# Preparation of a chunked RWKV-7 recurrence: the 64-row products of both heads and both halves ahead of the transposes

## The chip, the cores and the metric

The kernel runs on one core of a Trainium2 chip. The metric is device time of one execution in microseconds. Three executions of the kernel before took 3186.7, 3193.28 and 3202.15 us; the median is 3193.28 us.

## The reference

A decoder trunk of two layers on a 1024 x 1024 input. Layer 0 mixes tokens with a gated MLP, layer 1 with an RWKV-7 recurrence; each is followed by cross-attention into 256 memory rows and a SwiGLU FFN, and every sub-layer is wrapped in RMS norms. The change lies in the recurrence of layer 1, with 16 heads of 64:

```python
def rwkv7_recurrence(r, w, k, v, a, b):
    def step(S, inp):
        r_t, w_t, k_t, v_t, a_t, b_t = inp
        sa = jnp.einsum('bhij,bhj->bhi', S, a_t)
        S = S * w_t[:, :, None, :] + sa[..., None] * b_t[:, :, None, :] + v_t[..., None] * k_t[:, :, None, :]
        return S, jnp.einsum('bhij,bhj->bhi', S, r_t)
    ...
    _, y = lax.scan(step, S0, xs)
    return jnp.moveaxis(y, 0, 1)
...
def rwkv7_time_mix(x, v_first, mix, w_rkv, w0, w1, w2, a0, a1, a2, g1, g2, k_k, k_a, r_k, ln_g, ln_b, w_o, v_res):
    xm = x[None] + xx[None] * mix[:, None, None, :]
    r, k, v = jnp.einsum('pbtc,pcd->pbtd', xm[:3], w_rkv)
    ...
    decay = jnp.exp(-jnp.exp(heads(w)))
    y = rwkv7_recurrence(rh, decay, kh, vh, -kk, kk * ah)
    ...
    return (y * g) @ w_o, v_first
```

## The kernel before

Everything is float32. The large projections split an operand into a rounded part and a remainder and run three 128x512 matmuls for one product (lines L148 to L150, called "triples" below); splitting costs a cast on ACT (L118) and a subtraction on DVE (L119).

The recurrence is cut into chunks of 64 positions and done in four batches of 256 positions. A batch goes through these stages:

- `rwkv_prep` (L1313 to L1389), once for each of four groups of channels (`pi` 0 to 3). It loads five tiles (L1325), accumulates decays on DVE (L1328), takes exponentials on ACT, and builds two operand tiles AR and BK (L1340 to L1344). Partitions 0 to 63 belong to one head of a pair, 64 to 127 to the other. A group has 8 chunks of 64, taken in two halves `q` of four. For each half and head, four products of 64 rows go into one PSUM bank (L1363), and DVE masks the bank into GA and GR with two multiplications (L1366). Four 128x128 transposes of BK go into another bank (L1370), and ACT copies it (L1371). Then GA is sent to DRAM (L1376, L1377), the values are loaded into UV (L1381), and 16 more products (L1387) follow, which ACT copies (L1388).
- `rwkv_solve`: 31 steps of two DVE operations (L1409, L1410) on what the four groups of the batch have written, read back into invA (L1399). The results go to DRAM (L1414, L1417).
- `rwkv_merge`: reads these results back (L1426 into x1, L1431 into Z) and joins them with 32x32 matmuls (L1443, L1452).
- `rwkv_chunks`: the recurrence itself (L1479, L1466), and `rwkv_post`, which normalises the outputs; its reductions are on DVE (L1531, L1544), its transposes on PE (L1553, L1560).

Batch 0 is prepared while the last half of a projection (`rwkv_cols`) runs, batch 1 while the gate projection (L1307) runs and beyond it, batches 2 and 3 between two runs of `rwkv_chunks`, beside the post-processing of the batch before. Merge b stands ahead of the preparation of batch b+1 in the source.

These functions are generators. Between two `yield`s a step is recorded, and `stagger` starts the four groups of a batch some steps apart (its second argument, 7 or 6 on L1592). A scheduler at build time then puts the recorded instructions of all stages into one order for each engine; on the chip an engine follows this order and waits at each instruction for its inputs and buffers. While batches are prepared, PSUM is split into four banks for `bank()` (used by the preparation and by the post-processing of the first two batches) and four for `bank_ck()` (merge and chunks).

Of the kernel before, what the change touches and what calls it, by code (L numbers as in the profile page):

```python
# [21 lines left out]
class Trunk:  # L22
# [1290 lines left out]
    def rwkv_prep(self, R, B, pi, b, d, C):  # L1313
# [13 lines left out]
        L, kkn, b, km, r = [ld[n] for n in ('sig', 'kkn', 'b', 'km', 'r')]  # L1327
# [29 lines left out]
        for q in range(2):  # L1357
            qs = slice(q * 4, q * 4 + 4)
            for h in range(2):
                hs = slice(h * 64, h * 64 + 64)  # L1360
                ps = self.bank()
                for c in range(4):
                    nc.tensor.matmul(ps[:, c * P:(c + 1) * P], lhsT=BK[hs, q * 4 + c, :, :], rhs=AR[hs, q * 4 + c, :, :], start=True, stop=True)  # L1363
                pv = ps.rearrange('p (c a t) -> p c a t', c=4, a=2)
                for a, x in ((0, GA), (1, T['GR'])):
                    nc.vector.tensor_mul(x[:, h, qs, :], pv[:, :, a, :], self.mask[:, a].broadcast_to([P, 4, 64]))  # L1366
                yield
            ps = self.bank()
            for c in range(4):
                nc.tensor.transpose(ps[:, c * P:(c + 1) * P], BK[:, q * 4 + c, :, :], self.ident)  # L1370
            nc.scalar.copy(T['BT'][:, qs, :], ps.rearrange('p (c t) -> p c t', c=4))  # L1371
            yield
# [193 lines left out]
    def rwkv(self, W, C, filler, mk_close):  # L1566
        nc = self.nc
        B = [self.rwkv_batch() for _ in range(4)]
        R, states = ({}, {})
# [6 lines left out]
        def stagger(gens, lag):  # L1576

            gens = list(gens)
            done = [False] * len(gens)
            n = 0  # L1580
            while not all(done):
                for i, g in enumerate(gens):
                    if n >= i * lag and (not done[i]):
                        try:
                            next(g)
                        except StopIteration:
                            done[i] = True
                n += 1
                yield

        def prep(b):
            return stagger([self.rwkv_prep(R, B[b], pi, b, D_[0], C) for pi in range(4)], 7 if b else 6)  # L1592

        def chunks(b):
            yield from self.rwkv_chunks(R, B[b], b, states)
# [17 lines left out]
        D_ = []  # L1613

        def before_last():
            self.close_main()
            pools(left, 'left', ('inv', 1), ('D', 8))
            self.rwkv_consts(left.enter_context(self.tc.tile_pool(name='rconst', bufs=1, reuse_waits='tile', side='left')), C)
            pools(left, 'left', ('ld', 7))
            pools(top, 'left', ('tt', 4))  # L1620
            self.open_main(2, 3, 2)
            self.open_psum(4, 4)
            self.later(prep(0))
        d, gate_out = self.rwkv_project(W, C, filler, before_last, D_)
        self.drain()
        run(self.rwkv_solve(R, B[0]))
        p1 = prep(1)
        self.later(p1)
        gate_out()
# [11 lines left out]
        for b in range(1, 4):  # L1641
            o = 3
            sv = self.rwkv_solve(R, B[b])
            if o in (0, 1):
                run(sv, chunks(b - 1))
            elif o in (2, 3):
                run(chunks(b - 1), sv)
            else:
                self.later(sv)
                run(chunks(b - 1), rate=1)  # L1650
                self.drain(0)
            self.later(post(b - 1), 1)
            if b == 3:
                break
            if o in (0, 2, 4):
                run(self.rwkv_merge(R, B[b]))
            run(prep(b + 1), rate=1)
            if o in (1, 3, 5):
                run(self.rwkv_merge(R, B[b]))
            self.drain()  # L1660
# [99 lines left out]
```

## Time and profile before

| what | value |
|---|---|
| median of three executions | 3193.28 us |
| the profiled execution, whole | 3190.62 us |
| its span in the profile | 3188.9 us |
| mean granted clock of TensorE | 0.969 |
| first and last L1363 product | 1689.9 and 2057.7 us |

A line of groups reads: line of the code, engine, operation, tile written <- tiles read, shapes, count, then busy time and mean duration, then the engine's idle time just before these instructions and what ended it. A float32 matmul leaves two records, so 8 records of L1363 are four products. A line of the timeline gives a start, the time to the end of the last merged record, the instruction, and in brackets the idle time ahead of it with what ended it. A line of windows gives a stretch and its length, then for each engine the busy time and number of records, then the granted clock (1.00 is full), the busy share of the DMA engines and GB/s.

### The profile page before, as it was taken

How to read it: one execution, taken by the hardware profiler on the slowest of the kernel's cores; microseconds unless marked ns; L12 is line 12 of the kernel's file. 1: busy time of each engine (PE TensorE's matmuls, PEld its weight loads, DVE VectorE, ACT ScalarE, POOL GpSimd, SP SyncE). 2: the span in 40 equal slices, each digit the busy share in tenths (PEclk: the TensorE clock that was granted, in tenths of full speed). 3: DMA queues.
4: the chain of work that ended last, by engine and by line, in shares of the span. 5: the costliest groups of instructions: out<-in, count | busy, mean ns of one | idle time of the engine just before them, and what ended most of it. 6: DMA issues, size and time to landing. Idle time of an engine off the chain costs nothing. (4 is left out here: it accounts for less than half of the span.)

```text
span 3188.9 us, 43900 instructions
## 1 busy us (share of the span) xinstructions
PE 3076.4 (96%) x16570; PEld 2519.2 (79%) x16570; DVE 1826.3 (57%) x2610; ACT 1484.8 (47%) x2751; POOL 796.7 (25%) x632
## 2 busy tenths in 40 slices
PE   8999999989999999999989999999999999999998
PEld 6888888778888877878767778787788778888877
DVE  5553544565555576655765665664545655555666
ACT  5443544533333345766653344455544633333443
POOL 0100011345555200111421120323011355554101
PEclk9999999999999999999998888899999999999999
DMA  5622535423333643744867632633643423333634
GB/s 191 207 79 67 195 116 166 163 73 100 100 102 100 234 160 131 226 125 147 263 194 197 187 94 81 174 97 128 206 152 130 148 93 108 103 100 106 228 125 142
DMA packets 434580, 457.60 MB, mean 143 GB/s; under 512 B 77696, under 2 KB 309280, under 8 KB 434368
## 3 DMA queue, kind: packets, MB, share of 16 engines
q1 hardware_dynamic: 427456, 429.62, 42.4%
q0 software_dynamic: 6912, 25.17, 2.5%
q8 instruction: 131, 2.15, 0.3%
q14 instruction: 81, 0.66, 0.1%
HBM read 332.48 MB, written 122.22 MB: 143 GB/s over the span
## 5 line engine op out<-in xcount | busy, mean ns | idle before, releaser
L461 PE MATMUL ps<-a,wh 128*128 128x512 f32 x2464 | 773.1, 399 | 7.8 <-DVE a L119 7.4
L119 DVE TENSOR_TENSOR wl<-wr,wh 128x1024 fp32r<-128x1024 f32 (+1 forms) x417 | 486.1, 1176 | 458.9 <-ACT wh L118 454.5
L118 ACT CAST wh<-wr 128x1024 fp32r<-128x1024 f32 (+1 forms) x417 | 371.1, 901 | 601.4 <-PE ps L671 168.1
L461 PEld LDWEIGHTS ps<-a,wh 128*128 128x128 f32 x2464 | 466.4, 190 | 123.2 <-DVE a L119 9.2
L461 PE MATMUL ps<-a,wl 128*128 128x512 f32 x1232 | 480.7, 398 | 0.9 <-DVE wl L119 0.9
L148 PE MATMUL ps<-a,wh 128*128 128x512 f32 (+1 forms) x848 | 329.5, 393 | 9.7 <-ACT a L118 7.4
L149 PE MATMUL ps<-a,wh 128*128 128x512 f32 (+1 forms) x848 | 326.3, 386 | 2.4 <-DVE a L119 2.4
L148 PE MATMUL ps<-wh,a 128*128 128x512 f32 x800 | 314.9, 402 | 13.4 <-ACT t L1201 4.0
L150 PE MATMUL ps<-a,wl 128*128 128x512 f32 (+1 forms) x848 | 325.3, 385 | 2.3 <-DVE wl L119 2.2
L149 PE MATMUL ps<-wl,a 128*128 128x512 f32 x800 | 318.8, 399 | 0.5 <-DVE wl L119 0.5
L150 PE MATMUL ps<-wh,a 128*128 128x512 f32 x800 | 316.7, 399 | 0.0
L220 POOL TENSOR_TENSOR sm<-sm,mhalf 128x2 f32<-128x2 f32 (+3 forms) x68 | 70.8, 1045 | 902.8 <-DVE sm L240 827.0
L461 PEld LDWEIGHTS ps<-a,wl 128*128 128x128 f32 x1232 | 233.4, 189 | 57.8 <-DVE wl L119 1.3
L119 DVE TENSOR_TENSOR wl<-s,wh 128x512 fp32r<-128x512 f32 (+1 forms) x188 | 201.6, 1087 | 73.9 <-ACT wh L118 70.8
L671 PE MATMUL ps<-wl,wh 128*128 128x512 f32 x588 | 231.6, 394 | 11.5 <-DVE wl L119 11.3
L671 PE MATMUL ps<-wh,wl 128*128 128x512 f32 x588 | 230.0, 391 | 0.0
L118 ACT CAST wh<-s 128x512 fp32r<-128x512 f32 (+1 forms) x188 | 115.5, 633 | 207.9 <-PE ps L461 75.2
L148 PEld LDWEIGHTS ps<-a,wh 128*128 128x128 f32 x848 | 162.6, 193 | 43.7 <-ACT a L118 8.4
L671 PE MATMUL ps<-wh 128*128 128x512 f32 x588 | 194.3, 391 | 0.0
L150 PEld LDWEIGHTS ps<-a,wl 128*128 128x128 f32 x848 | 163.0, 193 | 37.1 <-DVE wl L119 4.0
L148 PEld LDWEIGHTS ps<-wh,a 128*128 128x128 f32 x800 | 151.7, 190 | 50.7 <-ACT t L1201 4.5
L149 PEld LDWEIGHTS ps<-a,wh 128*128 128x128 f32 x848 | 163.4, 193 | 33.0 <-DVE a L119 2.7
(289 smaller groups left out, 5284.7 us busy)
## 6 DMA issues: line engine op xcount, KB each, us to landing
scr<-a SPq DMA_DIRECT2D x218, 256.0 KB
wr<-in_ffn_w_in SPq DMA_DIRECT2D x92, 512.0 KB
wr<-scr SPq DMA_DIRECT2D x70, 512.0 KB
scr<-t SPq DMA_DIRECT2D x58, 512.0 KB
wr<-in_rw_w_rkv SPq DMA_DIRECT2D x48, 512.0 KB
a<-in_ffn_w_out SPq DMA_DIRECT2D x36, 512.0 KB
ld<-scr SPq DMA_DIRECT2D x72, 256.0 KB
t<-scr SPq DMA_DIRECT2D x34, 512.0 KB
```

Source lines behind the costliest of these rows:

```text
L118: self.nc.scalar.copy(hi, src)
L119: (engine or self.nc.vector).tensor_sub(lo, src, hi)
L148: nc.tensor.matmul(out, lhsT=ah, rhs=bh, start=start, stop=False)
L149: nc.tensor.matmul(out, lhsT=ah, rhs=bl, start=False, stop=False)
L150: nc.tensor.matmul(out, lhsT=al, rhs=bh, start=False, stop=stop)
L220: self.nc.gpsimd.tensor_tensor(out=r, in0=v, in1=self.mhalf[:, 0:n], op=ALU.pow)
L461: self.nc.tensor.matmul(out, lhsT=a, rhs=b, start=start and k == 0 and (i == 0), stop=k == 3 and i == 2, skip_group_check=True)
L671: nc.tensor.matmul(ps, lhsT=a, rhs=b, start=i in (1, 2, 5) and n == 0 and k == 0 and z == 0, stop=n == NS - 1 and k == steps[n][1] - 1 and ...
```

## The change

Two edits. The `yield` between the two heads of a half goes out of the loop over heads, and the loop over halves is cut in two: first the products of both halves, one step each with both heads, then the transposes of both halves, one step each. A group so has two steps fewer, and the distance between groups in `stagger` goes from 7 and 6 steps to 6 and 5. No instruction is added or taken away.

```diff
@@ rwkv_prep
                 pv = ps.rearrange('p (c a t) -> p c a t', c=4, a=2)
                 for a, x in ((0, GA), (1, T['GR'])):
                     nc.vector.tensor_mul(x[:, h, qs, :], pv[:, :, a, :], self.mask[:, a].broadcast_to([P, 4, 64]))
-                yield
+            yield
+        for q in range(2):
+            qs = slice(q * 4, q * 4 + 4)
             ps = self.bank()
             for c in range(4):
                 nc.tensor.transpose(ps[:, c * P:(c + 1) * P], BK[:, q * 4 + c, :, :], self.ident)
@@ rwkv
         def prep(b):
-            return stagger([self.rwkv_prep(R, B[b], pi, b, D_[0], C) for pi in range(4)], 7 if b else 6)
+            return stagger([self.rwkv_prep(R, B[b], pi, b, D_[0], C) for pi in range(4)], 6 if b else 5)
```

Behind L1367 a line of the changed kernel has a number higher by 2 (the transposes L1370 are L1372 there, the merge products L1443 are L1445). The scheduler's order changes on every engine, from the preparation of batch 0 on. Three places show it.

On PE, the third group of batch 3 before the change, from its first small products on (`ck` with L1452 is the merge of the batch before, `bk` and `ar` are BK and AR):

```order
L1351 MATMUL ps<-sel,ld 128x2 x4
L1387 MATMUL ps<-uv,bk 64x64 x7
L1363 MATMUL ps<-ar,bk 128x128 x8
L1370 MATMUL ps<-ident,bk 128x128 x4
L1452 MATMUL ck<-z_14071,x1t 32x32 x2
L1452 MATMUL ck<-z_14072,x1t 32x32
L1363 MATMUL ps<-ar,bk 128x128 x4
L1452 MATMUL ck<-z_14072,x1t 32x32
L1452 MATMUL ck<-z_14071,x1t 32x32
L1363 MATMUL ps<-ar,bk 128x128 x4
```

and the same group after it:

```order
L1389 MATMUL ps<-uv,bk 64x64 x16
L1351 MATMUL ps<-sel,ld 128x2 x4
L1363 MATMUL ps<-ar,bk 128x128 x16
L1372 MATMUL ps<-ident,bk 128x128 x4
L1454 MATMUL ck<-z_14133,x1t 32x32
L1454 MATMUL ck<-z_14134,x1t 32x32 x2
L1454 MATMUL ck<-z_14133,x1t 32x32
L1372 MATMUL ps<-ident,bk 128x128 x4
```

What was a row of 8 products (both heads of a half) and two rows of 4 (one head each) is one row of 16. Over the whole program there are 28 rows of 4 and 18 of 8 before, so 18 places where four products of one head stand next to four of the other. After, there are 40 such places; by batch they go from 5, 5, 4, 4 to 11, 9, 8, 12.

On DVE, the solve of batch 0 before the change, where the preparation of batch 1 cuts in:

```order
L1409 TENSOR_TENSOR invP<-invZ,invA 128x135
L1410 TENSOR_TENSOR invZ<-invZ,invP 128x5x27
L1340 SCALAR_TENSOR_TENSOR ar<-ld,tt 128x8x63
L1341 TENSOR_SCALAR ar<-ld 128x8
L1342 TENSOR_TENSOR ar<-ld,tt 128x8x64
L1343 TENSOR_TENSOR bk<-ld,tt 128x8x64
L1409 TENSOR_TENSOR invP<-invZ,invA 128x156
```

and after it:

```order
L1412 TENSOR_TENSOR invZ<-invZ,invP 128x11x21
L1411 TENSOR_TENSOR invP<-invZ,invA 128x240
L1340 SCALAR_TENSOR_TENSOR ar<-ld,tt 128x8x63
L1341 TENSOR_SCALAR ar<-ld 128x8
L1342 TENSOR_TENSOR ar<-ld,tt 128x8x64
L1412 TENSOR_TENSOR invZ<-invZ,invP 128x12x20
```

Five of the 31 steps stood ahead of the first operand of batch 1; now eleven and a half do. On PE, the 16 last products of batch 0 (L1387) had 75 matmuls of triples behind them before the gate projection; now they have 99.

On PE, the first merge before the change (L1307 is the last of the gate projection, `x_14093` the solve's result as read back into x1):

```order
L1307 MATMUL ps<-a 128x512
L1363 MATMUL ps<-ar,bk 128x128 x4
L1370 MATMUL ps<-ident,bk 128x128 x4
L1387 MATMUL ps<-uv,bk 64x64 x16
L1443 MATMUL ck<-x_14093 32x32 x64
L1351 MATMUL ps<-sel,ld 128x2 x4
L1363 MATMUL ps<-ar,bk 128x128 x8
```

and after it:

```order
L1307 MATMUL ps<-a 128x512
L1389 MATMUL ps<-uv,bk 64x64 x8
L1351 MATMUL ps<-sel,ld 128x2 x4
L1363 MATMUL ps<-ar,bk 128x128 x8
L1445 MATMUL ck<-x_14155 32x32
L1363 MATMUL ps<-ar,bk 128x128 x8
L1445 MATMUL ck<-x_14155 32x32 x63
L1372 MATMUL ps<-ident,bk 128x128 x8
```

The merge now has the first products (L1351) and the first half of the third group of batch 1 ahead of it; before, it came first. In batch 3 the merge now stands behind the whole product blocks of two groups, where it stood behind half a block of the first. In batch 2 it stands directly behind the product block of the first group, ahead of the transposes of the post-processing, of which three rows came first before.

## The prediction

> **What bounds the kernel now.** I read the engines' shares first, then the stretches in which batches are prepared, then the preparation's instructions one by one. First the page, then windows over batch 0, batch 2, batch 3 and one piece of batch 2:
>
> ```profile
> PE 3076.4 (96%) x16570; PEld 2519.2 (79%) x16570; DVE 1826.3 (57%) x2610; ACT 1484.8 (47%) x2751; POOL 796.7 (25%) x632
> ...
> 1692.50:1750.00 57.50, 56.89 (x389) 47.53 (x389) 32.43 (x62) 20.38 (x37) 8.18 (x7) 0.89 0.74 187
> ...
> 1889.00:1956.00 67.00, 61.36 (x592) 52.39 (x592) 39.27 (x89) 23.23 (x46) 22.19 (x19) 0.64 0.56 153
> 2005.00:2058.00 53.00, 48.87 (x568) 41.63 (x568) 31.49 (x75) 18.96 (x39) 19.78 (x18) 0.77 0.72 198
> ...
> 1930.00:1960.00 30.00, 30.00 (x250) 26.80 (x251) 12.91 (x31) 10.39 (x23) 3.20 (x4) 0.60 0.41 108
> ```
>
> PE is busy 96% of the span, and nearly all of the preparation too: 56.89 of 57.5 us in batch 0, 61.36 of 67 and 48.87 of 53 in batches 2 and 3. DVE is busy 56 to 59% there. So PE's own issue sets the pace, and what it is spared counts. The granted clock matters as much: batches 2 and 3 do about the same work, and take 67 us at 0.64 and 53 us at 0.77.
>
> The groups of 1680 to 2070 us, on DVE and PE, say who waits for whom:
>
> ```profile
> L1363 PE MATMUL ps<-ar,bk 64*128 64x128 f32 x512 | 82.8, 336 | 3.1 <-DVE sm L1544 1.4 <-ACT bo L1353 1.0 <-ACT t L1308 0.6
> L1366 DVE TENSOR_TENSOR bk<-ps,mask 128x256 f32<-128x256 f32 x64 | 26.7, 417 | 64.5 <-PE ps L1363 64.4
> ...
> L1328 DVE TENSOR_TENSOR_SCAN ld<-chunk_on,ld 128x512 f32<-128x512 bf16 x16 | 19.5, 1218 | 19.9 <-DMA ld<-scr 19.9
> ```
>
> DVE is idle for 64.4 us until L1363 delivers, while L1363 itself waits 3.1 us in all. The products are what DVE waits for.
>
> **Change, part 1: two heads side by side.** PE's timeline has one block of both heads (16 records), and a block of one head (8), each with the row that starts next, first at full clock and then at half:
>
> ```profile
> 1700.06 1.71 PE L1363 MATMUL ps<-ar,bk 64*128 64x128 f32 x16
> 1701.70 0.66 PE L1370 MATMUL ps<-ident,bk 128*128 128x128 f32 x4
> ...
> 1705.52 1.16 PE L1363 MATMUL ps<-ar,bk 64*128 64x128 f32 x8
> 1706.60 1.15 PE L1387 MATMUL ps<-uv,bk 128*64 128x64 f32 x16
> ...
> 1811.31 3.10 PE L1363 MATMUL ps<-ar,bk 64*128 64x128 f32 x16
> 1814.33 1.11 PE L1370 MATMUL ps<-ident,bk 128*128 128x128 f32 x4
> ...
> 1832.07 2.08 PE L1363 MATMUL ps<-ar,bk 64*128 64x128 f32 x8
> 1834.08 0.79 PE L1479 MATMUL ck<-s,ar 128*128 128x128 f32 x2
> ```
>
> From start to next start, one head takes 1.08 us, both 1.64. Two separate blocks would take 2.16, so each neighbourhood of two heads spares 0.52 us at full clock. At half clock it is 2 x 2.01 - 3.02 = 1.00. The products use different rows of the array and overlap where the head changes; a block also enters and leaves its shape once instead of twice.
>
> The built orders have 18 such neighbourhoods before and 40 after, 6, 4, 4 and 8 more in batches 0 to 3. That the one from the second head back to the first spares the same is an assumption; no row of before has it.
> Batch 0 at a clock of 0.89: 6 x 0.52 = 3.1. For batches 2 and 3, a clock of 0.64 means 0.72 of the time at half, 0.77 means 0.46, which gives 0.87 and 0.74 us each: 4 x 0.87 = 3.5 and 8 x 0.74 = 5.9. Batch 1 I put at 0.75: 3.0. Of the first group of batches 2 and 3, two each lie beside a wait of PE for the post-processing (part 3) and bring nothing: +3.2. Sum -12.3, call it **-12**. Bounds: 0, if other waits cover all of it, and 22 x 1.00 = -22, if all runs at half clock.
>
> [...]
>
> **Part 2: the merges' waits.** L1443, asked by its line, and its first start in merges 0 and 1:
>
> ```profile
>   DMA x<-scr: 10.4, 4
> ...
> 1807.65 1.93 PE L1443 MATMUL ck<-x 32*32 32x32 f32 x128 [4.34 <-DMA x<-scr]
> ...
> 1902.35 0.55 PE L1443 MATMUL ck<-x 32*32 32x32 f32 x24 [1.96 <-DMA x<-scr]
> ...
> 1803.27 0.88 DVE L1348 SCALAR_TENSOR_TENSOR ld<-ld,pcol 128x256 f32<-128x256 f32 x2 [1.16 <-POOL bk L1344]
> ```
>
> Merge 0 waits 4.34 us for the solve's result. The solve ran here, its start released by the read-back of GA; the triples that I count in have the spacing of the last two rows:
>
> ```profile
> 1751.94 0.19 DVE L1409 TENSOR_TENSOR invP<-invZ,invA 128x31 f32<-128x31 f32 x1 [1.34 <-DMA invA<-scr]
> ...
> 1797.96 0.21 DVE L1410 TENSOR_TENSOR invZ<-invZ,invP 128x31 f32<-128x31 f32 x1
> ...
> 1709.72 0.40 PE L150 MATMUL ps<-a,wl 128*128 128x512 f32 x1
> 1709.96 0.39 PE L148 MATMUL ps<-a,wh 128*128 128x512 f32 x1
> ```
>
> In the new order 24 more matmuls of triples stand behind batch 0's last product, at 0.24 us each 5.6 us. The solve starts that much earlier against the projection, and more of its steps stand ahead of batch 1 on DVE. So the 4.34 us go. Next is the third group of batch 1, now ahead of the merge: its last operand comes from DVE at 1804.15 (1803.27 + 0.88, L1348), while PE was through at 1803.31 (1807.65 - 4.34). I keep 0.8 us and take -3.5. Merge 2 moves behind two whole blocks; I give it half of what the other two waits have left (10.4 - 4.34 - 1.96 = 4.1, about 2 each): -1. Merge 1 moves ahead of three blocks of transposes of the post-processing, which no longer cover its wait (3.3 us, by the 1.1 of such a block of four in part 3); but its solve starts earlier by what batch 1 gains. I take 0, between -2 and +3.3. Together **-4.5**, between -8.3 (4.34 + 2 + 2) and +3.3. The DMAs of GA and UV keep their places behind each group's last mask, so SP has as many issues; POOL's L1344 keeps its place ahead of the products.
>
> **Part 3: banks.** Four products now want all four banks of the pool in one go, the transposes a fifth. DVE empties a bank at this pace:
>
> ```profile
> 1745.15 0.41 DVE L1366 TENSOR_TENSOR gr<-ps,mask 128x256 f32<-128x256 f32 x1
> 1745.48 0.42 DVE L1366 TENSOR_TENSOR bk<-ps,mask 128x256 f32<-128x256 f32 x1
> 1745.82 0.41 DVE L1366 TENSOR_TENSOR gr<-ps,mask 128x256 f32<-128x256 f32 x1
> ```
>
> 0.67 us for a pair. PE makes a bank in 1.08 us, and each further one in 0.56 (1.64 - 1.08), so four in 2.76; the first is free again at about 1.7. With DVE ready there is a slack of 1 us. Where it isn't, at the start of batches 2 and 3, the post-processing's reduction holds banks already:
>
> ```profile
>   DVE sm L1544: 9.1, 4
> ...
> 1898.22 1.12 PE L1370 MATMUL ps<-ident,bk 128*128 128x128 f32 x4 [2.19 <-DVE sm L1544]
> ```
>
> The transposes wait 2.19 us there (9.1 in four places). It will be the second half's products instead. I add 1.1 us in each of the two batches, **+2**, between 0 and 4.4.
>
> **Sum:** -12 - 4.5 + 2 = -14.5 us, on the profiled execution of 3190.62 (span 3188.9) 3176. That execution lies 2.7 us under the median of 3193.28, from which the same sum gives **3179**. A measurement here tells 0.5%, 16 us, from no change, so the boundary is 3177.
>
> **Rivals.**
>
> *The clock stays up.* The half clock lasts long here: the windows show 0.60 at 1930 to 1960 with PE busy 30.00 of 30. Denser products and shorter waits may turn one stretch back to full. At 0.64, batch 2 has 48 us of half clock; half of that at full saves 24 x (1 - 1.08/2.01) = 11 us, in both batches up to 22: 3168 to 3157. Against it: products of half the array's rows and 32x32 matmuls remain. [...]
>
> *The clock falls instead.* Batch 3 in the state of batch 2 costs 67 - 53 = 14 us: 3193.
>
> *It is covered.* Loads come next: DVE waits 19.9 us for `ld<-scr` already, at L1328, and that pool doesn't grow. If faster groups only wait for their loads and the solves, part 1 is given back: about 3190. For it, the DMA share of 0.74 in batch 0; against it, DVE's 64.4 us of waiting for products.
>
> *Banks hold PE up, and the kernel is slower.* Each of the 16 groups pays the wait that the transposes paid for L1544, 9.1/4 = 2.3 us: 37 us, hence 3216. It decides from DVE being more than the 1 us of slack late in most groups, behind solve steps and operand building. If only half the groups pay, 3197. Against it: DVE is the one that waits now.
>
> **How the numbers follow.** Forecast 0.45, its own range 3168 to 3189; clock up 0.20; covered 0.20; clock down 0.05; banks 0.10. Nearly half of the forecast's own range lies beyond the boundary: faster 0.20 + 0.22 = 0.42, slower 0.10, same 0.48. The range leaves out the banks' case and a little of the clock's best: 3158 to 3200.
>
> **What would show it.** Part 1: blocks of 32 records of L1363 in about 2.8 us at full clock, some 5.0 at half, and DVE's 64.4 us of waiting shrunk. Part 2: L1443's 10.4 us of DMA waits cut by about half, the first from 4.34 to under 1. Part 3: few waits of L1363 and the transposes for L1366. The clock rivals show in the granted clock of the windows of batches 2 and 3. I am wrong if a block of 32 takes 3.3 us or more at full clock, or if waits for `ld<-scr` or L1366 grow by 10 us.

## The result and the profile after

The changed kernel takes 3209.58 us (median of 10 executions, 3192.89 to 3217.0), the kernel before 3194.47 us in the same comparison (10 executions). The ratio is 1.0054, with a 95% interval of 1.0032 to 1.0075: slower by about half a per cent, where 14.5 us less was forecast. The profiled execution took 3210.66 us (span 3208.6), 20.0 us more than that of before.

The engines' shares on the page are nearly what they were:

```profile
PE 3070.8 (96%) x16570; PEld 2519.6 (79%) x16570; DVE 1832.7 (57%) x2610; ACT 1485.1 (46%) x2751; POOL 793.6 (25%) x632
```

PE is busy 5.6 us less than before in a span that is 19.7 us longer. The difference shows where the recurrence runs. Windows from the first product L1363 to the last transpose of the post-processing (L1553, now L1555), before and after; the numbers behind the stretch are its length and PE's busy time, and further on stands the granted clock:

```profile
1689.90:2213.90 524.00, 502.79 (x4844) 423.24 (x4844) 312.06 (x759) 246.74 (x639) 115.34 (x111) 0.87 0.47 132
```

```profile
1694.80:2233.20 538.40, 494.32 (x4845) 421.33 (x4845) 315.96 (x759) 247.49 (x639) 114.89 (x111) 0.85 0.45 128
```

The stretch grew by 14.4 us. PE's idle time in it went from 21.2 us (524.00 - 502.79) to 44.1 us, and its busy time fell by 8.5 us although more of it ran at half clock: by the clock records of the two traces, 133 us of the stretch before and 157 us after. (Another 4.9 us of the 20 arose ahead of the first product, where PE's order of instructions is the same in both kernels; that part is not the change's, and the medians differ by 15.1 us.)

What PE waited for, by the waits between 1680 and 2240 us, longest first (total, times, longest), before and after:

```profile
PE ck L1443 <- DMA x<-scr: 8.1, 3, 4.3
PE ps L1370 <- DVE sm L1544: 4.2, 2, 2.2
...
PE ps L1387 <- DMA uv<-scr: 0.2, 1, 0.2
```

```profile
PE ps L1389 <- DMA uv<-scr: 25.5, 9, 5.8
PE ps L1351 <- DVE ld L1348: 5.9, 2, 4.1
PE ps L1555 <- DVE gr L1366: 4.1, 2, 3.9
```

The new first line is the largest of what is new: the products of GA with UV (L1387, now L1389) wait 25.5 us for UV's load, which they practically never did before. The same group of channels in both kernels, the last of batch 0, shows how. Timeline of before, SP's DMAs and PE (SPq is SP's queue):

```profile
1737.84 1.25 SPq L1381 DMA_DIRECT2D uv<-scr  x2
...
1743.62 1.71 PE L1363 MATMUL ps<-ar,bk 64*128 64x128 f32 x16
...
1745.93 0.86 SPq L1376 DMA_DIRECT2D scr<-bk  x2
...
1746.83 0.58 SPq L1377 DMA_DIRECT2D scr<-bk  x1
1748.42 2.08 PE L1387 MATMUL ps<-uv,bk 128*64 128x64 f32 x32
```

and after:

```profile
1747.29 2.26 PE L1363 MATMUL ps<-ar,bk 64*128 64x128 f32 x24
...
1749.29 0.58 SPq L1383 DMA_DIRECT2D uv<-scr  x1
1749.48 1.09 PE L1372 MATMUL ps<-ident,bk 128*128 128x128 f32 x8
...
1750.44 0.41 DVE L1366 TENSOR_TENSOR gr<-ps,mask 128x256 f32<-128x256 f32 x1
1750.55 0.85 SPq L1378 DMA_DIRECT2D scr<-bk  x2
1751.45 0.60 SPq L1379 DMA_DIRECT2D scr<-bk  x1
1752.09 0.63 SPq L1383 DMA_DIRECT2D uv<-scr  x1
1754.05 3.55 PE L1389 MATMUL ps<-uv,bk 128*64 128x64 f32 x32 [3.47 <-DMA uv<-scr]
```

Before, both loads of UV were issued 8.1 us ahead of the first write of GA, although the source has them behind it: the scheduler puts them there, and they land while products, masks and transposes run. After, the first load leaves 1.3 us ahead of the writes, the second behind them. The masks are through at 1750.85, and PE stands until 1754.05, 4.2 us after the first load was issued. In the trace of before, all 16 pairs of loads stand ahead of their group's writes; after, in 3 groups both do, in 6 one, in 7 none. From the end of a load's issue to the first product that reads it there were 7.7 us on the median of the 32 loads before, and under 4.2 us for 2 of them; after it is 3.5 us, and under 4.2 for 20. (4.2 is what the load above took. The nine loads that PE waited for were used 2.2 to 4.3 us after their issue, so not every load under 4.2 is one that PE waits for.)

The granted clock fell in such a wait as well. In the clock records of this trace the granted clock is 1.00 or 0.50, and every stretch between two changes of it lasts a multiple of 3.41 us (the shortest 3.41, the longest 628.05). Five such windows of the changed kernel around another of these waits (1731.6 to 1734.54, 2.94 us):

```profile
1726.63:1730.04 3.41, 3.41 (x41) 3.33 (x40) 1.63 (x6) 1.65 (x5) 0.00 (x0) 1.00 0.71 203
1730.04:1733.45 3.41, 1.56 (x13) 1.20 (x12) 3.41 (x9) 1.07 (x2) 0.00 (x0) 1.00 1.07 260
1733.45:1736.87 3.42, 2.33 (x17) 2.24 (x18) 0.90 (x3) 0.29 (x1) 0.00 (x0) 0.50 0.73 194
1736.87:1740.28 3.41, 3.41 (x9) 2.64 (x9) 1.22 (x1) 1.03 (x3) 0.00 (x0) 0.50 0.29 100
1740.28:1743.69 3.41, 3.41 (x15) 2.49 (x14) 0.17 (x1) 0.40 (x1) 0.00 (x0) 1.00 0.26 77
```

In the second window PE is busy 1.56 of 3.41 us; the next two run at 0.50, the second of them with PE busy throughout. That one holds 9 records, the window at full clock behind it 15.

### The profile page after: what moved, and what is told of

It is laid out like the page before. It is cut to its first block, busy times and chain, and to the rows that moved or that the text cites. A ratio compares the mean times of both kernels' runs of the same rounds, so it can differ in the third digit from the quotient of the medians.

```text
span 3208.6 us, 43910 instructions
## 1 busy us (share of the span) xinstructions
PE 3070.8 (96%) x16570; PEld 2519.6 (79%) x16570; DVE 1832.7 (57%) x2610; ACT 1485.1 (46%) x2751; POOL 793.6 (25%) x632
## 4 chain that ended last, share of the span: by engine, by line
PE 81%; DVE 8%; DMA 6%; ACT 2%; issue 2%; SPq 1%; POOL 1%; DVEq 0%; POOLq 0%; ACTq 0%
PE ps L461 26%; PE ps L148 11%; PE ps L150 11%; PE ps L149 11%; PE ps L671 10%; PE ck L1468 4%; DVE wl L119 2%; PE ck L1481 2%; DVE a L119 1%; PE ps L1389 1%; PE ps L1363 1%; DMA uv<-scr 1%; DMA a<-scr 1%; DMA ld<-scr 1%; PE ps L274 1%
## 5 line engine op out<-in xcount | busy, mean ns | idle before, releaser
L148 PE MATMUL ps<-wh,a 128*128 128x512 f32 x800 | 315.6, 402 | 14.4 <-DVE a L432 4.8
L149 PEld LDWEIGHTS ps<-a,wh 128*128 128x128 f32 x848 | 163.3, 193 | 33.2 <-DVE a L119 2.7
```

What stands on the lines that cost most here:

```text
L148: nc.tensor.matmul(out, lhsT=ah, rhs=bh, start=start, stop=False)
L149: nc.tensor.matmul(out, lhsT=ah, rhs=bl, start=False, stop=False)
```

## The experiments

Three theories stand in the expectations of the first eight. U: the late loads of UV are what the changed order costs. S: it is the shift of the whole order, in which waits of many kinds replace each other. H, in e1 and e2 alone: it is the longer half clock by itself. The theories 1 to 3 and M of the later runs are told in their expectations. Each kernel was timed against the kernel before on the same chip (medians of before in the four sets: 3188.86, 3190.73, 3187.52 and 3189.1 us). In the table, "late loads" are those of the 32 with under 4.2 us from issue to use, "waits for UV" are PE's in the profiled execution, and the half clock is the mean over all timed executions, 2 x (1 - mean clock) x span in each.

| kernel | median us | ratio to before, 95% interval | late loads | waits for UV, us | half clock, us |
|---|---|---|---|---|---|
| before (90 executions) | | | 2 | 0.2 | 193 |
| the change | 3209.58 | 1.0054 [1.0032, 1.0075] | 20 | 25.5 | 215 |
| e1 change, loads ahead of the products | 3196.47 | 1.0018 [0.9996, 1.0039] | 2 | 1.8 | 206 |
| e2 before, loads ahead of the products | 3195.63 | 1.0029 [1.0007, 1.0052] | 0 | 0 | 209 |
| e3 heads joined only | 3209.16 | 1.0062 [1.0041, 1.0083] | 2 | 5.0 | 229 |
| e4 loops split only | 3224.7 | 1.0103 [1.0070, 1.0136] | 16 | 15.0 | 246 |
| e5 change, loads just ahead of GA's writes | 3227.7 | 1.0111 [1.0088, 1.0135] | 14 | 19.6 | 237 |
| e6 as e1, heads alternating | 3193.17 | 1.0007 [0.9988, 1.0026] | 2 | 1.2 | 201 |
| e7 change, distances 7 and 6 | 3205.89 | 1.0039 [1.0016, 1.0061] | 16 | 8.5 | 218 |
| e8 before, distances 6 and 5 | 3229.29 | 1.0112 [1.0077, 1.0147] | 7 | 15.1 | 252 |
| e9 change, matmuls added ahead of L1389 | 3201.63 | 1.0041 [1.0019, 1.0063] | 11 | 5.6 | 166 |
| e10 change, loads between products and transposes | 3193.48 | 1.0024 [1.0005, 1.0044] | 5 | 2.8 | 208 |
| e11 as e1, distances 7 and 6 | 3212.23 | 1.0082 [1.0057, 1.0106] | 0 | 0 | 243 |
| e12 as e6, distances 7 and 6 | 3213.17 | 1.0081 [1.0059, 1.0102] | 0 | 2.1 | 238 |
| e13 before, the same matmuls added | 3213.26 | 1.0078 [1.0050, 1.0105] | 2 | 0 | 189 |
| e14 as e10, one matmul added | 3200.92 | 1.0039 [1.0015, 1.0063] | 0 | 6.1 | 180 |

### The loads moved, in both kernels (e1, e2)

```diff
+        UV = T['UV'] = self.A.tile([P, 8, 2, 64], F32, name='uv', tag='a')
+        nc.gpsimd.memset(UV[0:64], 0.0)
+        for p in range(2):
+            nc.sync.dma_start(UV[64:128, p * 4:p * 4 + 4].rearrange('i c h v -> i c (h v)'), ...)
         for q in range(2):
             qs = slice(q * 4, q * 4 + 4)
             for h in range(2):
...
             nc.sync.dma_start(B['D1'][bl, pi].rearrange('h c i t -> i (h c) t'), ga[s, :, s])
         nc.sync.dma_start(B['D4'][pi].rearrange('i h c t -> i (h c) t'), ga[0:32, :, 32:64])
-        UV = T['UV'] = ...
```

> The changed kernel with the UV tile, its memset and its two loads recorded ahead of the products instead of behind the writes of GA. Theory U (the second UV load leaves SP's queue behind the GA writes, which wait for the last mask, so that L1389 waits on PE): the waits of L1389 for uv<-scr fall from 25.5 us to under 4, PE idle in the preparation falls by about 20 us, and the time is below the kernel before by 5 to 20 us, ratio 0.994 to 0.998. Theory H (the longer half clock of TensorE alone makes the loss): the waits go, the time stays at a ratio of 1.003 or more. Theory S (any new order of the scheduler scatters by this much): no relation between the waits and the time.

> The kernel before with the same move of the UV loads. Before, L1387 waited 0.2 us for them, so theories U and H expect no change: ratio 0.997 to 1.003. Theory S expects a change of either sign of up to 0.5%.

With the loads early, the changed order is no longer told from before (1.0018), and it is not slower than the old order with the same move (1.0029). PE's waits for UV are gone but for 1.8 us. They are not the whole story: U expected 5 to 20 us less than before. The products are denser (L1367 is busy 63.8 us in e1, the same line L1363 82.8 in the kernel before), but PE's idle time in the stretch is still 37.0 us, against 44.1 in the changed kernel and 21.2 before. Other waits have taken the place of most of the 24 us. Longest waits of PE in e1 (L1370 is the masks here, L1376 the transposes):

```profile
PE ck L1445 <- DMA x<-scr: 10.9, 3, 5.3
PE ps L1376 <- DVE gr L1370: 6.4, 3, 5.5
PE ps L1389 <- DVE a L1563: 5.1, 2, 4.3
PE ps L1389 <- DVE gr L1370: 4.8, 3, 3.7
...
PE ps L1389 <- DMA uv<-scr: 1.8, 2, 1.1
```

PE now waits 11.2 us for DVE's masks and 10.9 us for the solve's result. H expected 1.003 or more for e1; its interval doesn't exclude that, and half clock fell too, from 215 to 206 us.

### Half of the change (e3, e4) and the distances alone (e7, e8)

e3 takes the `yield` out between the heads and leaves the transposes behind their half, with the new distances 6 and 5; e4 splits the loop over halves and leaves the `yield`, with the old distances 7 and 6:

```diff
# e3
-                yield
+            yield
             ps = self.bank()
...
# e4
                 yield
+        for q in range(2):
+            qs = slice(q * 4, q * 4 + 4)
             ps = self.bank()
```

> Only the first edit: both heads of a half in one step, the transposes still behind their half, distances 6 and 5. Theory U: the transposes of the second half still follow its products, and L1387 follows the transposes, as before; waits for uv<-scr stay between the two, 5 to 15 us, and the time is within 0.4% of before. If joining the heads alone makes the loss, the ratio is 1.004 or more.

> Only the second edit: all products first and the transposes behind, with a yield after each head and the distances 7 and 6 of before. Theory U: the last mask comes earlier against L1387 by a block of transposes, so the waits for uv<-scr are under 10 us; ratio 0.997 to 1.003. If moving the transposes makes the loss, waits of 15 us or more and a ratio of 1.004 or more.

It is the split that makes the loads late (16 in e4, 2 in e3). Both are slower all the same, e3 with hardly a late load. U missed in both: it expected them within 0.4 and 0.3% of before, and under 10 us of waits for UV in e4, which has 15.0. e7 is the change with the old distances between groups, e8 the kernel before with the new ones:

```diff
# e7
-            return stagger([...], 6 if b else 5)
+            return stagger([...], 7 if b else 6)
# e8
-            return stagger([...], 7 if b else 6)
+            return stagger([...], 6 if b else 5)
```

> The changed kernel with the distances between groups of before (7 and 6). If the tighter distance causes the crowding of products against the UV loads, the waits for uv<-scr fall below 12 us and the ratio to 1.002. Theory U puts the cause inside a group (products, transposes, loads in that order), so the waits stay at 15 to 30 us and the ratio at 1.003 to 1.008.

> The kernel before with the distances of the change (6 and 5) alone. A control for what a new order of the scheduler does by itself: theory U expects 0.998 to 1.003 and waits for uv<-scr under 5 us. If such a shift alone gives 1.005, scatter of the order explains the change as well as any wait does.

The distances by themselves, with no other edit, cost the kernel before 1.1%. Its waits in e8:

```profile
PE ps L1387 <- DMA uv<-scr: 15.1, 4, 6.4
PE ck L1443 <- DMA x<-scr: 9.4, 2, 6.4
```

Four long waits for UV are part of it, and half clock is 252 us, the most of all kernels. U did not expect this, S did. In the changed kernel the old distances bring no more than 0.15 points, which the intervals don't separate, although PE's waits for UV fall from 25.5 to 8.5 us in e7. U had expected 15 to 30 us there. PE's idle time in the stretch stays at 40.0 us, so other waits replaced these, as S says.

### The loads just ahead of GA's writes (e5), and the heads alternating (e6)

e5 exchanges the four lines of UV with the five of GA's writes. e6 is e1 with the products of both heads issued in turn into two banks:

```diff
+            pss = [self.bank() for _ in range(2)]
+            for c in range(4):
+                for h in range(2):
+                    hs = slice(h * 64, h * 64 + 64)
+                    nc.tensor.matmul(pss[h][:, c * P:(c + 1) * P], lhsT=BK[hs, q * 4 + c, :, :], rhs=AR[hs, q * 4 + c, :, :], start=True, stop=True)
```

> The changed kernel with the UV tile, memset and loads just ahead of the three writes of GA, at the same step; nothing else. It takes the last mask and SP's three issues (about 1.6 us) from between the products and the second UV load. Theory U: the waits of L1389 for uv<-scr fall from 25.5 us to under 10, and the ratio from 1.0054 to 1.001 to 1.003, as with the loads ahead of the products (1.0018). If the loads are late because the values themselves or the tile come late, the waits stay above 20 us and the ratio at 1.005.

> The changed kernel with the UV loads ahead of the products, and with the heads alternating product by product (h0, h1, h0, h1) into two banks instead of four of one and four of the other. If row halves overlap at every change of head, a block of 32 records takes 1.5 to 2.1 us at full clock instead of 2.75, 16 groups spare 10 to 20 us of PE, and the ratio is 0.994 to 1.000 against 1.0018 with the loads alone. If the overlap comes only from entering the block, the block stays at 2.7 us and the ratio at 1.002.

e5 was a miss: 1.0111. The scheduler kept both loads ahead of the writes in 9 groups only, in batch 0 by 1.3 to 2.6 us, and put both behind the first write in the other 7, so 14 stay late and 19.6 us of waits remain. Why it is slower than the change itself is not explained by that. e6 has the lowest ratio of all variants, and is not told from before. Alternating did make the products denser where the built order kept it. Two rows of 16 records in e6, each with the row that starts next, at full clock:

```profile
2031.54 1.71 PE L1367 MATMUL ps<-ar,bk 64*128 64x128 f32 x16
2033.18 0.24 PE L1446 MATMUL ck<-x 32*32 32x32 f32 x2
2033.36 1.17 PE L1367 MATMUL ps<-ar,bk 64*128 64x128 f32 x16
2034.45 0.22 PE L1446 MATMUL ck<-x 32*32 32x32 f32 x2
```

The first takes 1.64 us like the rows of the changed kernel: its records start at the same distances as there, so it has four products of one head and four of the other. The second takes 1.09 us: its records start in pairs 13 ns apart, one of each half as in the source. By this spacing about half of e6's 30 rows have runs of one head only, as the scheduler built them, and in all the products of e6 are busy 60.8 us, those of e1 63.8. Little of that could show in the total.

### Filling the wait (e9), its control (e13), and loads a little earlier (e10, e14)

e9 adds two matmuls per group ahead of the products that wait; their result is overwritten:

```diff
             ps = self.bank()
+            if q == 0:
+                for _ in range(2):
+                    nc.tensor.matmul(ps, lhsT=self.ident, rhs=BK[:, 0:4, :, :], start=True, stop=True)
             for c in range(4):
```

> The changed kernel, with two added matmuls of 128x512 f32 per group on TensorE right ahead of L1389's first block (their bank is overwritten by that block; they read BK and write nothing that is kept). They depend on nothing that is late, so they fill the time in which L1389 waits for its UV load. By the blocks of four 128x128 f32 records (1.08 us) I estimate 1.1 us each, 16 x 2.2 = 35 us of added work. Theory 1 (a wait also costs clock: in nine traces, every 3.41 us window at full clock with TensorE busy under half was followed by half clock): waits for uv fall from 25.5 to under 8, half clock between the first product and the last L1555 falls from 157 to 125 us or less, and of the 35 us at least 25 come back: 1.004 to 1.009 against before. Theory 2 (half clock comes from the many small products, not from the waits): waits fall too, half clock stays at 150 us or more, time 1.010 to 1.014.

e13 is the same edit in the kernel before:

> The kernel before with the same two added matmuls per group at the same place, ahead of the first block that needs UV. It has no waits for UV to fill (0.2 us). Theory 1 (in the changed kernel the fill helped because it stood in the waits): here the added work is paid in full; with half clock at 193 us per execution on the mean before, and 215 to 166 by the fill in the changed kernel, I expect 175 us or more here and 1.006 to 1.011 against before, which is over the changed kernel with the fill (1.0041). Theory 3 (full-array matmuls anywhere in this stretch hold the clock up, waits or not): half clock falls by 40 us or more here too, and the time is 1.002 to 1.006.

The added records in the view by groups (busy time, mean ns, idle time ahead), in e9 and in e13:

```profile
L1388 PE MATMUL ps<-bk,ident 128*128 128x512 f32 x64 | 33.2, 643 | 0.7 <-DVE gr L1366 0.6
```

```profile
L1386 PE MATMUL ps<-bk,ident 128*128 128x512 f32 x64 | 36.0, 692 | 0.0
```

The stretch from the first product to the last transpose of the post-processing as a window, in e9 and in e13:

```profile
1689.40:2222.70 533.30, 507.79 (x4908) 413.21 (x4909) 316.96 (x759) 248.50 (x639) 117.70 (x111) 0.91 0.45 130
```

```profile
1693.00:2232.00 539.00, 525.66 (x4906) 425.73 (x4906) 315.44 (x760) 247.46 (x638) 118.39 (x111) 0.90 0.46 128
```

The same 33 to 36 us of added matmuls cost the kernel before 24 us (1.0078) and the changed kernel nothing (1.0041 against 1.0054). Each ratio is good to some 0.2 points, 7 us. In the changed kernel they stand where PE waited: 25.5 us of waits for UV became 5.6, PE's idle time in the stretch fell from 44.1 to 25.5 us, and half clock over all executions from 215 to 166 us. In the kernel before half clock went from 193 to 189: there the added matmuls did not hold the clock up by themselves, though its one profiled execution has 0.90 in this stretch, a high one. That speaks for the waits as the source of the half clock that e9 took away; e14 speaks against it.

e10 puts the four lines of UV between the two loops, e14 adds one such matmul to e10:

> The changed kernel with the UV tile, its memset and its loads recorded between the products and the transposes: an earlier place than in the changed kernel, a later one than ahead of the products. Theory U (the late load is what the changed order costs): the median from the issue's end to the first use, 3.5 us in the changed kernel and 16.5 with the loads ahead of the products, comes to 5 to 9 us; waits for uv 3 to 12 us; time between the two, 1.001 to 1.004. Theory S (the order of the whole stretch decides, the load is one wait among others that replace each other): waits for uv fall as well, but the time stays at 1.005 or more.

> UV loads between products and transposes as in e10 (1.0024), with one added matmul per group, about 18 us of work. Theory 1: few waits for UV are left to fill (2.8 us), so the added work is not got back: 1.003 to 1.008, half clock 190 us or more per execution on the mean. Theory 3: half clock to 175 us or less and 0.999 to 1.003.

e10 has 7.6 us from issue to use on the median, like the kernel before, 5 late loads, and 1.0024. Two places for the loads so agree: of the 0.54% that the change costs, taking the late loads away gives back 0.30 to 0.36 points, each good to 0.3 points. S, which expected 1.005 or more for e10, missed here. The filler of e14 is 20.1 us of work:

```profile
L1388 PE MATMUL ps<-bk,ident 128*128 128x512 f32 x32 | 20.1, 715 | 1.3 <-DVE gr L1366 1.2
```

It costs 0.15 points, 5 us, although e10 had only 2.8 us of waits for UV to fill (e14 has 6.1), and half clock fell from 208 to 180, where 190 or more was expected. So added matmuls can take half clock away where they fill hardly any of these waits, and how much of e9's fall came from its waits stays open. By the ratios and half clocks of the table, at 0.385 us for each microsecond of half clock (worked out below), the fillers cost about 15 of 33.2 us in e9, 26 of 36.0 in e13 and 16 of 20.1 in e14 when the clock is taken out. By that some 10 us of e9's filler disappeared in the waits, an estimate no surer than the ratios.

### Longer distances with early loads (e11, e12)

e11 is e1, e12 is e6, both with the distances 7 and 6. They were tried as versions that might beat both kernels:

> Loads of UV ahead of the products as in e1, and the lags between the groups back at 7 and 6. Theory M (with the loads early, what holds TensorE is the masks: all four banks of a half are filled before a mask is through, and nothing of another group stands between; 6.4 and 4.8 us in e1): a longer lag puts more of other groups' work between, waits for the masks L1370 fall to under 6 in all, time 0.996 to 1.001. Theory S: waits move elsewhere (the merges' x, the solve), 1.001 to 1.006.

> As e11, with the two heads' products alternating one by one as in e6 (the best of the variants at equal clock). Theory M: waits for the masks L1371 fall from 12.9 to under 6, time 0.995 to 1.000: the one variant that could beat both kernels. Theory S: 1.000 to 1.005.

Theory M missed: PE's waits for the masks are under 6 us in e11 as it expected (3.7), in e12 they are not (12.9, as in e6), and neither kernel gained. Both lose 0.8% with no late load, at 240 us of half clock. So other orders of the same instructions cost as much without any wait for UV. What in them does so was not taken apart. No version was found that beats the kernel before.

## Why the prediction was wrong, point by point

**The step that failed** is the one that was costed at nothing: "The DMAs of GA and UV keep their places behind each group's last mask, so SP has as many issues". The count was right and the places were not. They are not behind the last mask before the change: the scheduler had put all 16 pairs of UV's loads ahead, 8.1 us ahead of GA's writes in the group shown. In the changed order 13 groups have at least one load behind the writes. The source's order was taken for SP's. SP's timeline of the kernel before shows otherwise in its own rows, as at 1776.20 for a pair of loads and 1781.68 for its group's first write, and the prediction uses none of them. The wait that this opened is 25.5 us against 0.2, about 25 us that no rival named, and PE's idle time in the stretch rose by 22.9 us, where the prediction had it fall by 2.5. e1 and e10 take the wait away and give back 0.36 and 0.30 points; e9 fills it and takes up 33 us of added work at no cost, where the old order pays 24, though part of that came by the clock. What the wait costs by itself is known no better than that, because in e1 and e7 other waits took its place.

**The clock** was weighed as two rivals, up at 0.20 and down at 0.05; shorter waits were to bring it up, and longer ones were not considered. The unlikely one came true in batch 3. Windows of 2005 to 2070 us, before and after (the first number behind the counts is the granted clock):

```profile
2005.00:2070.00 65.00, 59.71 (x686) 50.71 (x686) 38.02 (x94) 26.62 (x58) 19.91 (x18) 0.82 0.67 184
```

```profile
2005.00:2070.00 65.00, 51.12 (x575) 46.82 (x576) 39.12 (x88) 18.66 (x38) 19.56 (x16) 0.66 0.56 158
```

Over 230 timed executions of the sixteen kernels, with one constant for each kernel, the time rises by 0.385 us for each microsecond of half clock (scatter 2.8 us). From 193 to 215 us that makes 8.5 us of the change's cost. The rest is rough: 10 us against the four sets of the kernel before whose clocks are on record, 6.6 against the medians of the comparison itself (15.1 - 8.5). In the windows above, 6.83 us at 0.50 (1733.45 to 1740.28) began within PE's wait of 2.94 us (1731.6 to 1734.54).

**Part 1 was right in mechanism and price.** Blocks of 32 records, each with the row that starts next, at full and at half clock:

```profile
1727.75 2.82 PE L1363 MATMUL ps<-ar,bk 64*128 64x128 f32 x32
...
1730.50 1.10 PE L1372 MATMUL ps<-ident,bk 128*128 128x128 f32 x8
...
2051.07 5.13 PE L1363 MATMUL ps<-ar,bk 64*128 64x128 f32 x32
...
2056.14 1.11 PE L1372 MATMUL ps<-ident,bk 128*128 128x128 f32 x4
```

They take 2.75 and 5.07 us, where 2.8 and 5.0 were expected; the step from the second head back to the first spares as much as the other. The line of the products agrees. Before it was busy for 82.8 us, and in the change it has

```profile
L1363 PE MATMUL ps<-ar,bk 64*128 64x128 f32 x512 | 69.9, 345 | 3.0 <-ACT bo L1353 2.0 <-DVE sm L1546 0.5 <-DVE gr L1366 0.5
```

12.9 us less, where -12 was forecast, although a record took a little longer on the mean (345 ns, 336 before). In the block at 1727.75 records of one head start 111 to 112 ns apart, and at each of the three changes of head three pairs of records start 4 to 6 ns apart: that is the overlap. Entering and leaving the shape shows as well, as 214 ns from the first record to the second and 203 ns from the last to the transposes. The price belongs to an order that has each head's products in a run of four, as the row of 1.64 us has. In turn, 16 records took 1.09 us in e6, about half of 2 x 1.08, an order that the change doesn't have.

What was spared on PE was paid back as waiting. DVE's wait hardly shrank, and the loads of `ld` took more:

```profile
L1366 DVE TENSOR_TENSOR bk<-ps,mask 128x256 f32<-128x256 f32 x64 | 26.7, 417 | 61.2 <-PE ps L1363 61.2
...
L1328 DVE TENSOR_TENSOR_SCAN ld<-chunk_on,ld 128x512 f32<-128x512 bf16 x16 | 20.9, 1307 | 29.0 <-DMA ld<-scr 29.0
```

64.4 us became 61.2, and 19.9 became 29.0: the covered rival was partly true as well. Of the signs that the prediction set for being wrong none came (a block of 3.3 us or more, waits for `ld` or the masks longer by 10 us): it watched other places than the one that failed.

**Part 2 was right in kind, and undersized.** L1445, asked by its line, and in PE's own waits, has

```profile
  DMA x<-scr: 2.5, 2
...
PE ck L1445 <- DMA x<-scr: 1.1, 1, 1.1
```

for 10.4 and 8.1 before. The view of a line adds the waits of weight loads (PEld), which run beside PE's, so the prediction's 10.4 counts 2.4 us twice. On PE alone it is 7.0 us where 4.5 were expected. Merge 0 does not wait any more. (24 triples at 0.24 us are 5.8 us, not 5.6; nothing hangs on that.)

**Part 3 and the rival of the banks.** Part 3 did not come in its form. Here too the prediction's 9.1 us in four places are 4.2 us of PE in two and 5.0 of weight loads. PE's waits for the post-processing's reduction (4.2 us at the transposes, 1.4 at the products) fell to 0.5 us instead of moving to the products. In their place the post-processing's L1555 waits 4.1 us for the masks and the products 0.5. That is 5.8 us before with L1553's 0.2, and 5.1 after, so the term was about nothing, at the lower end of its bounds of 0 to 4.4, and the rival's 37 us did not come. That its 3216 lies nearest to the measured time is luck. In e1 the masks do hold PE up (11.2 us), and then at the transposes and the UV products behind the products.

What stays open is why e3, e5, e8, e11 and e12 lose 0.6 to 1.1%. They have from 0 to 14 late loads, and all have 229 us of half clock or more; U alone doesn't explain them, and S says no more than that each order leaves other waits. It also stays open why the scheduler moved the loads.

## What to carry to other kernels

Where a scheduler sets the order, read the order of the DMA queue too: a load that the source records behind a write may have been issued 8 us ahead of it, and a regrouping of matmuls can take that lead away. Count for each load the time from issue to first use before and after, since one that was never waited for shows in no wait of the old profile. A wait of TensorE of two or three microseconds is to be priced with the half clock that can follow it (here 6.83 us at 0.50, begun within a wait of 2.94 us). A wait taken away is not yet time gained, since the next one may stand behind it: compare the engine's whole idle time. And a few microseconds spared on an engine that is 96% busy are kept only if nothing that it waits for moves closer.

## What the runs showed of the hardware

- Over the sixteen traces, in the stretch from the first product to the last transpose of the post-processing: of the 3.41 us windows at full clock with PE busy under half of the time, 59 of 59 were followed by half clock; with PE busy 50 to 90%, 62 of 172; with 90% or more, 36 of 1602. In the example one window with 1.85 us of idle time (3.41 - 1.56) stood ahead of half clock.
- Half clock also stayed behind busy windows: of the 564 windows of the same stretches at half clock with PE busy 90% or more, 394 were followed by another at half clock.
- Products of the two row halves overlapped where the half changed: 16 records at full clock took 1.64 us with one change in the middle, and 1.09 us with the halves in turn (e6); one half alone took 1.08 us for 8.
